# One hybrid decoder layer: the order of the recurrence heads and the distance of the attention's score runs are changed

## The chip, the cores and the metric

The kernel runs on one NeuronCore of a Trainium2 chip. The metric is the device time of one execution in microseconds (us). Three runs of the kernel before gave 470.46, 470.69 and 470.61 us, median 470.61 us. Five engines work side by side: TensorE (PE: matmuls into PSUM, its weight loads shown as PEld), VectorE (DVE), ScalarE (ACT), GpSimd (POOL) and SyncE (SP). Each takes its instructions in a fixed order and waits at the head of its queue.

## The reference

One layer on 512 tokens of width 1024. The normalised input goes through one wide projection, whose columns feed two branches.

- **Attention** (`aq`, `ak`, `av`, `ag`): 8 heads of 64. Queries and keys are normalised per head; scores get a bias that depends on the distance, then a causal softmax. With 512 tokens and blocks of 256, a query sees every earlier key, so that all causal keys count. The result is gated with `silu(ag)`.
- **Recurrence** (`bq`, `bf`, `bi`, `bg`): 4 heads with keys and values of 128. The sigmoid-like forget gate gives a log decay per token and channel; `cum` is its running sum. In chunks, with decay handled inside each score:

```python
    o_inter = jnp.einsum('bhtk,bhkv->bhtv', qc * jnp.exp(cum), state)
    scores = jnp.einsum('bhtk,bhsk,bhtsk->bhts', qc, kc, jnp.exp(diff))
    o_intra = jnp.einsum('bhts,bhsv->bhtv', scores, vc)
    state = state * jnp.exp(last[:, :, 0, :, None]) + jnp.einsum('bhsk,bhsv->bhkv', kc * jnp.exp(last - cum), vc)
```

  The output is normalised per head and gated with `silu(bg)`.

Each branch is projected up to 1024 columns, the two are merged with the sigmoids of `gate_a` and `gate_b`, projected once more and added to the input; then a gated embedding is added.

## The kernel before, in words

**Numbers.** Every product of two fp32 operands is made as three matmuls in a faster fp32 form: both operands are split into a high and a low part (`split`, lines 192 to 194: ScalarE writes the high part, VectorE the difference), and high-high, high-low and low-high are added up. The weights are loaded in blocks, split two blocks ahead of their use (`LD = 2`), and there are two raw buffers and three of each part.

**The order on TensorE is written out.** The program's order is TensorE's order (`manual_schedule`). The other engines' orders come from the scheduler's own simulation; `in_order` marks a few VectorE operations that keep the program's order among themselves, and `high_priority(offset=AHEAD)` moves others forward. The main sequence is the projections: values `bi`, `av`, head 0's `bf` and `bq`, then `aq`, `ak`, then the list `ORDER` (gate blocks `bg`, `ag`, `ga`, `gb` and the other heads' `bf`, `bq`), ending in eight blocks `ub` (up-projection of the recurrence, L252); then `ua` (of the attention), `h` (output projection), `g` and `pe` (gated embedding).

**Side work between the products.** The recurrence and the attention are Python generators. A clock `now` in planned us advances by 0.681 for three matmuls of 512 columns (`tick`) and by `cost` for side work. A generator yields a distance in us or a condition, and goes on at the first tick at which this is met. So the yields decide between which products a step stands on TensorE.

**The recurrence of one head.** `hgrn_gates` makes keys, queries and `cum` behind the head's two projections. `hgrn_intra` (from L484) makes the scores inside chunks of 128. They are cut into levels: for blocks of size b, decayed tiles `hx` (function `kq`, on VectorE and ScalarE, with a yield of `HP = 2.5` after each) hold keys times a decay up to a middle point and queries times a decay from it. A first stage multiplies levels 64, 32, 1 and 16 into the PSUM banks `lpb` and `lpa`; a second stage multiplies levels 8, 4 and 2 into the same `lpa`. Ahead of each stage stands `beside_attention`: it waits until the attention has issued its next run of scores, or 30 us. Masks then gather the levels into the tile `sc`. `hgrn_out` (L591) transposes decayed keys (`hktp`, copied to `hkt` at L599), multiplies them with the values to states' increments (`hds`, L604), makes the states `st` on VectorE, and adds the output in the bank `hop` (L617 and L619). From there VectorE and ScalarE make `ho`: square, sums over the columns, inverse square root, scaling (L624 to L626). `hgrn_gated` multiplies with the gate and splits into `ybh` and `ybl`, which `ub` reads. `ub0` multiplies heads 0 to 3 in this order, three matmuls each. In `recurrence`, head h runs through `hgrn_intra` and `hgrn_out`; only then does head h+1 begin its `kq` tiles.

**PSUM.** Eight banks: three for tag `mm` (projections), three for `a` (scores), two for `g`, which serve `lpb`, `lpa`, `hktp`, `hds` and `hop` of all heads.

**The attention.** For each pair of heads there are two steps: step 0 handles the query blocks 0, 1 and 2, step 1 block 3. `scores` multiplies queries and keys (L708). VectorE adds the bias and finds the row's extreme (L720), ScalarE takes the exponential (L722) and scales (L724), VectorE transposes in 32 by 32 blocks (L727), and 16 DMAs from SP's queue (L738) sort the blocks into the transposed probabilities. These tiles lie in one buffer `pb` of eleven tiles: probabilities in 0 to 2, transposed ones from 3, sorted ones from 6 (step 0) and from 9 (step 1). `out_values` multiplies the sorted probabilities of both steps with the values into the bank `o` (L751), behind the scores of the next pair's step 0. `PACE` is the planned distance from one step's scores to the next: 14 behind step 0 and 27 behind step 1.

Of the kernel before, what the change touches and what calls it, by code (L numbers as in the profile page):

```python
# [28 lines left out]
LEVELS = (16, 8, 4, 2, 1)  # L29

STEPS = ((0, 1, 2), (3,))
PACE = (14.0, 27.0)

HP = 2.5
H0 = 8.0
# [22 lines left out]
def hybrid_layer_kernel(  # L58
# [23 lines left out]
    ctx.enter_context(tc.manual_schedule(engines=ENG))  # L82


    BUFS = {"w": 2, "wh": 3, "wl": 3, "A": 16, "X": 16, "YB": 8, "H": 12, "T": 3, "Q": 4, "KT": 2, "SG": 4, "VV": 8, "s32": 1, "st": 1, "ps": 8}

    def unit(tag, name, dt=F32, shape=(128, 512)):
        return sb.tile(list(shape), dt, tag=tag, bufs=BUFS[tag], name=name)
# [12 lines left out]
    def spawn(gen, after=0.0):  # L101
        sides.append([now[0] + after, gen])
# [44 lines left out]
            xr.append(t)  # L147


    pb = cst.tile([128, 11, 512], F32, name="pb")  # L150
    xfirst = pb[:, 0, 0:272]
    raw0 = unit("w", "wf0", shape=(128, 2, 512))
    A.preload_act_table_set("natural_log_exp_and_others")
# [329 lines left out]

    def hgrn_intra(h):  # L484
        kb, q, cum = hg[h]
        lpb = bank("g", f"lpb{h}").rearrange("p (l c t) -> p l c t", l=4, c=NT)
        big = lpb[:, 2:4].rearrange("p l c t -> p (l c t)").rearrange("p (c t) -> p c t", c=NT)

        def kq(b):

            x = unit("Q", f"hx{h}_{b}")
# [46 lines left out]
        k16 = kq(16)  # L538
        yield HP
        yield from beside_attention()  # L540
        lpa = bank("g", f"lpa{h}").rearrange("p (l c t) -> p l c t", l=4, c=NT)

        for c in range(NT):
# [46 lines left out]
    def hgrn_out(h, vb):  # L590
        kb, q, cum, kd = hg[h][:4]  # L591
        nk = 3 * 128
        yield 1.0
        kt = bank("g", f"hktp{h}")
        for c in range(3):
            PE.transpose(kt[:, c * 128:c * 128 + 128], kd[:, c * 128:c * 128 + 128], ident)
        cost(0.33)
        kts = unit("KT", f"hkt{h}")
        A.activation(kts[:, :nk], kt[:, :nk], AF.Copy)  # L599
        yield 2.5  # L600
        hv = slice(h * 128, h * 128 + 128)
        dsp = bank("g", f"hds{h}")
        for c in range(3):
            PE.matmul(dsp[:, c * 128:c * 128 + 128], kts[:, c * 128:c * 128 + 128], vb[c][:, hv],  # L604
                      start=True, stop=True)
        cost(0.65)
        st = unit("st", f"st{h}", shape=(128, 3, 128))
        V.tensor_copy(st[:, 0], dsp[:, 0:128])
        for c in (1, 2):
            e = c * 128 + 127  # L610
            V.scalar_tensor_tensor(st[:, c], st[:, c - 1], cum[:, e:e + 1], dsp[:, c * 128:c * 128 + 128],
                                   op0=OP.mult, op1=OP.add)
        yield 3.0
        op_ = bank("g", f"hop{h}")
        for c in range(NT):
            s_ = slice(c * 128, c * 128 + 128)
            PE.matmul(op_[:, s_], vb[c][:, hv], sc[:, c, :], start=True, stop=(c == 0))  # L617
            if c:
                PE.matmul(op_[:, s_], st[:, c - 1], q[:, s_], start=False, stop=True)  # L619
        cost(1.5)  # L620
        o = unit("YB", f"ho{h}")
        y = unit("Q", f"hy{h}")
        t = unit("Q", f"ht{h}")
        A.activation(t, op_, AF.Square)  # L624
        token_spread(y, token_factor(token_sums(t, unit("Q", f"htr{h}"), 1.0 / 128)))
        V.scalar_tensor_tensor(o, op_, ogain[:, h:h + 1], y, op0=OP.mult, op1=OP.mult)  # L626
        hg[h] += (o,)

    def hgrn_gated(h, sbg, res):
# [6 lines left out]
        res.append((h_, l_))  # L636
        done.add(f"yb{h}")

    def recurrence(vb, sbg, res):
        for h in range(GH):  # L640
            yield lambda: h in hg
            if h == 0:
                yield H0
            yield from hgrn_intra(h)
            yield from hgrn_out(h, vb)
            spawn(hgrn_gated(h, sbg, res))
            yield HP


    def qk_norm(name, banks, g, res):  # L650
        hs = [unit("A", f"{name}h{i}", R) for i in range(HPAIRS)]
        ls = [unit("A", f"{name}l{i}", R) for i in range(HPAIRS)]
        raws = []
        ss = cst.tile([128, NT, HEADS], F32, name=name + "ss")
        y = cst.tile([128, NT, HEADS], F32, name=name + "y")
        t_ = cst.tile([128, NT, HEADS], F32, name=name + "t")
        for t in range(NT):
            raw = pb[:, (0 if name == "q" else 4) + t]
            A.activation(raw, banks[t], AF.Copy)
            sq = pb[:, 8 + (t + (name == "k")) % 3]  # L660
            A.activation(sq, raw, AF.Square)
            V.tensor_reduce(ss[:, t], sq.rearrange("p (h d) -> p h d", h=HEADS), axis=AX.X, op=OP.add)
            raws.append(raw)
        V.tensor_scalar(ss, ss, 1.0 / 64, None, op0=OP.mult)
        rsqrt(y, t_, ss)
        for t in range(NT):
            r3 = raws[t].rearrange("p (h d) -> p h d", h=HEADS)
            V.tensor_tensor(r3, r3, y[:, t, :, None].to_broadcast([128, HEADS, 64]), op=OP.mult)
        yield 14.0
        for i in range(HPAIRS):  # L670
            tp = bank("a", f"{name}tp{i}")
            for t in range(NT):
                PE.transpose(tp[:, t * 128:t * 128 + 128], raws[t][:, i * 128:i * 128 + 128], ident)
            cost(0.44)
            with tc.high_priority(offset=AHEAD):
                scale_split(hs[i], ls[i], tp, g)
            res.append((hs[i], ls[i]))
            yield 1.3
        done.add(name)

    def attention(qn, kn, va, sags, res):
# [4 lines left out]
        def tiles(step):  # L686
            return 2 + (len(STEPS[step]) > 1)

        P0, Z0, PT0 = 0, 3, (6, 9)

        def scores(hp, step, T):
            (qh, ql), (kh, kl) = qn[hp], kn[hp]
            nt = tiles(step)

            sps = [bank("a", f"s{hp}{step}{i}") for i in range(nt)]
            extra = bank("mm", f"s{hp}{step}x") if nt > 2 else None

            def where(qb, j):
                b_, o = place(qb, j)
                return (extra, 0) if (qb, j) == (1, 1) else (sps[b_], o)  # L700

            for qb in STEPS[step]:
                nk = 128 * (qb + 1)
                for i in range(3):
                    for j in range(2):
                        js = slice(64 * j, 64 * j + 64)
                        b_, o = where(qb, j)
                        PE.matmul(b_[:, o:o + nk], (qh, ql, qh)[i][js, qb * 128:qb * 128 + 128], (kh, kh, kl)[i][js, :nk],  # L708
                                  start=(i == 0), stop=(i == 2))
            cost(sum(3 * max(0.107, (qb + 1) * 0.0538) for qb in STEPS[step]))  # L710
            z = pb[:, Z0:Z0 + nt].rearrange("p t f -> p (t f)").rearrange("p (b t f) -> p b t f", b=4, t=nt)
            with tc.high_priority(offset=AHEAD):
                left = [sum(place(qb, j)[0] == b for qb in STEPS[step] for j in range(2)) for b in range(nt)]
                for qb, j in [(qb, j) for qb in STEPS[step] for j in range(2)]:
                    b_, o = place(qb, j)
                    nk = 128 * (qb + 1)
                    p_ = pb[:, P0 + b_, o:o + nk]
                    st = unit("ps", f"ps{hp}{qb}{j}", shape=(128, 4))
                    s_, so = where(qb, j)
                    in_order(V.tensor_tensor_reduce(p_, s_[:, so:so + nk], T[j][:, nk - 1::-1], -1.0, 3e38,  # L720
                                                    OP.add, OP.min, st[:, 0:1]))
                    A.activation(p_, p_, AF.Exp, bias=st[:, 0:1], scale=-1.0, accum_out=st[:, 1:2])  # L722
                    V.reciprocal(st[:, 2:3], st[:, 1:2])
                    A.activation(p_, p_, AF.Copy, scale=st[:, 2:3])  # L724
                    left[b_] -= 1
                    if left[b_] == 0:
                        V.transpose(z[:, :, b_, :].rearrange("p b (n c) -> p b n c", c=32),  # L727
                                    pb[:, P0 + b_].rearrange("p (n b c) -> p b n c", b=4, c=32))
            return z

        def sorted_groups(step, z):
# [37 lines left out]
        for n in range(len(steps) + 1):  # L769
            if n >= 1:  # L770
                yield PACE[steps[n - 1][1]]
            if n < len(steps):
                hp, i = steps[n]
                if i == 0:
                    for j in range(2):
                        t = unit("T", f"bias{hp}{j}")
                        row = ed[2 * hp + j:2 * hp + j + 1, :]
                        nc.sync.dma_start(t, bass.AP(tensor=row.tensor, offset=row.offset,
                                                     ap=[[1, 128], [1, 512]]))
                        T[hp, j] = t  # L780
                z = scores(hp, i, [T[hp, 0], T[hp, 1]])
            if n >= 1 and steps[n - 1][1] == NS - 1:
                ho = steps[n - 1][0]
                while f"ag{ho}" not in done:
                    yield lambda: f"ag{ho}" in done
                out_values(ho, [pts.pop(n - NS + i_) for i_ in range(NS)])
            if n < len(steps):
                pts[n] = sorted_groups(i, z)
            runs[0] += 1
        runs[0] += 1000  # L790

# [242 lines left out]
```

## Time and profile before

| what | value |
|---|---|
| median of 3 runs | 470.61 us |
| the profiled execution, its own time | 470.31 us |
| its span, first to last instruction | 468.5 us |
| granted TensorE clock, mean | 0.992 |
| TensorE busy | 458.0 us (98%) |
| VectorE busy | 298.8 us (64%) |
| ScalarE busy | 277.0 us (59%) |
| `hop` of heads 1, 2, 3 at | 195.6, 259.7, 307.5 us |
| `ub0` begins at | 313.2 us |

The profile is of one execution. Some 1.8 us of its time lie outside the span. A row of a timeline gives start, duration, engine, line, operation, output and inputs; a bracket at its end gives the idle time just before it and what ended that. The duration of a matmul is longer than the distance to the next, since matmuls overlap. A row of the view by stretches gives the stretch, its length, busy time and number of instructions of each engine shown, then the granted clock, the share of the DMA engines and GB/s.

### The profile page before, as it was taken

Reading aid. Unit: us, or ns where it says so; the run is one execution under the profiler, and the core shown is the slowest. Engines: PE = TensorE matmul, PEld = TensorE weight load, DVE = VectorE, ACT = ScalarE, POOL = GpSimd, SP = SyncE. Lnnn points to the kernel's source line nnn. Section 1 sums busy time; section 2 is a strip of 40 time slices with the busy share of each in tenths; the row PEclk is TensorE's granted clock in tenths of the full one; section 3 lists DMA queues with packets and bytes.
Section 4 is the critical chain, followed back from the end, with each engine's and each line's share of the span. In section 5 each row is a group of like instructions: output and inputs, shape, how many; then the busy total and the mean of one; then the engine's idle time right before and its main releaser. Section 6 shows DMA issues by size and latency. Waiting matters only on the chain.

```text
span 468.5 us, 8111 instructions
## 1 busy us (share of the span) xinstructions
PE 458.0 (98%) x3106; PEld 378.3 (81%) x3106; DVE 298.8 (64%) x604; ACT 277.0 (59%) x532; POOL 38.4 (8%) x77
## 2 busy tenths in 40 slices
PE   9999999999999999999998999997999999999996
PEld 8888888788888888878886888776888788888886
DVE  5668684868798874679495499434559844554222
ACT  5758564657689985888697689763325522232201
POOL 0000100100000010001000000000111100000000
PEclk9999999999999999999999999997999999999999
DMA  7732233222322642344326331631233544322211
GB/s 249 280 99 92 96 128 91 91 91 71 111 80 69 190 138 91 92 123 153 108 67 192 105 112 45 186 110 45 77 104 136 200 145 152 105 86 100 91 45 45
DMA packets 23590, 53.72 MB, mean 115 GB/s; under 512 B 4352, under 2 KB 9728, under 8 KB 23552
## 3 DMA queue, kind: packets, MB, share of 16 engines
q0 software_dynamic: 9056, 32.51, 21.2%
q1 hardware_dynamic: 14352, 20.70, 14.5%
q8 instruction: 24, 0.39, 0.3%
q14 instruction: 14, 0.11, 0.1%
q10 hardware_dynamic: 144, 0.01, 0.0%
HBM read 45.86 MB, written 2.10 MB: 102 GB/s over the span
## 4 chain that ended last, share of the span: by engine, by line
PE 75%; issue 14%; DMA 4%; ACT 4%; DVE 2%; POOL 1%; POOLq 0%; ACTq 0%; DVEq 0%
PE g L252 9%; PE h L252 8%; PE ga L252 6%; PE ub L252 5%; PE ak L382 5%; PE aq L382 5%; PE av L382 5%; PE gb L252 5%; PE bi L382 4%; PE bf L252 4%; PE bq L252 4%; PE bg L252 2%; PE pe L252 2%; PE ag L252 2%; DMA wf<-in_w_tr_dram 2%
## 5 line engine op out<-in xcount | busy, mean ns | idle before, releaser
L193 ACT ACTIVATE wh<-wf 128x1024 fp32r<-128x1024 f32 (+1 forms) x78 | 75.6, 970 | 103.7 <-PE g L252 20.9
L194 DVE TENSOR_TENSOR wl<-wf,wh 128x1024 fp32r<-128x1024 f32 (+1 forms) x78 | 86.5, 1110 | 57.9 <-ACT wh L193 54.1
L226 POOL DMA_DIRECT2D wf<-in_w_tr_dram x30 | 15.8, 528 | 175.1 <-DVE wl L194 152.6
L252 PE MATMUL g<-hh,wh 128*128 128x512 f32 (+1 forms) x72 | 26.3, 366 | 0.0
L252 PE MATMUL g<-hl,wh 128*128 128x512 f32 (+1 forms) x72 | 26.3, 366 | 0.0
L252 PE MATMUL g<-hh,wl 128*128 128x512 f32 (+1 forms) x72 | 26.3, 366 | 0.0
L252 PE MATMUL ga<-xh,wh 128*128 128x512 f32 x64 | 25.7, 402 | 0.0
L252 PE MATMUL gb<-xh,wh 128*128 128x512 f32 x64 | 25.2, 394 | 0.0
L252 PE MATMUL h<-ml,wh 128*128 128x512 f32 x64 | 25.0, 391 | 0.1
L252 PE MATMUL ga<-xl,wh 128*128 128x512 f32 x64 | 25.0, 391 | 0.0
L252 PE MATMUL ga<-xh,wl 128*128 128x512 f32 x64 | 25.0, 390 | 0.0
L252 PE MATMUL gb<-xh,wl 128*128 128x512 f32 x64 | 24.9, 390 | 0.0
L252 PE MATMUL gb<-xl,wh 128*128 128x512 f32 x64 | 24.9, 389 | 0.0
L252 PE MATMUL h<-mh,wh 128*128 128x512 f32 x64 | 24.9, 389 | 0.0
L252 PE MATMUL h<-mh,wl 128*128 128x512 f32 x64 | 24.9, 389 | 0.0
L722 ACT ACTIVATE pb<-pb,ps 128x128 f32<-128x128 f32 (+3 forms) x32 | 17.6, 552 | 10.6 <-DVE ps L720 10.6
L720 DVE CUSTOM_DVE_ANT_0 pb<-s,bias 128x128 f32<-128x128 f32 (+3 forms) x28 | 12.8, 496 | 10.4 <-PE s L708 10.4
L921 DVE TENSOR_TENSOR hf<-h,xres 128x512 f32<-128x512 f32 x8 | 5.5, 692 | 18.0 <-PE h L252 18.0
L252 PE MATMUL ub<-ybh,wh 128*128 128x512 f32 x32 | 13.7, 428 | 3.4 <-ACT ybh L193 3.4
L724 ACT ACTIVATE pb<-pb,ps 128x128 f32<-128x128 f32 (+3 forms) x32 | 15.7, 550 | 0.0
L500 ACT ACTIVATE hx<-hx 128x512 f32<-128x512 f32 x24 | 14.6, 622 | 1.4 <-DVE hx L499 1.3
L252 PEld LDWEIGHTS g<-hh,wh 128*128 128x128 f32 x72 | 13.6, 189 | 2.2
(343 smaller groups left out, 1257.3 us busy)
## 6 DMA issues: line engine op xcount, KB each, us to landing
wf<-in_w_tr_dram POOLq DMA_DIRECT2D x30, 512.0 KB, 3.8
wf<-in_w_tok_dram POOLq DMA_DIRECT2D x8, 512.0 KB, 4.5
wf<-in_w_up_dram POOLq DMA_DIRECT2D x16, 256.0 KB, 2.9
wf<-in_w_o_dram POOLq DMA_DIRECT2D x8, 512.0 KB, 3.7
wf<-in_w_g_dram POOLq DMA_DIRECT2D x8, 512.0 KB, 3.6
wf<-in_w_tok_dram SPq DMA_DIRECT2D x6, 512.0 KB, 3.6
pb<-pb SPq DMA_DIRECT2D x64, 48.0 KB, 2.3
bias<-in_ed_dram SPq DMA_DIRECT2D x8, 256.0 KB, 3.4
```

The lines of the kernel that those rows point to most:

```text
L193: A.activation(hi, src, AF.Copy)
L194: V.tensor_tensor(lo, src, hi.bitcast(F32), op=OP.subtract)
L226: (G if len(wraw) >= FAR else nc.sync).dma_start(raw, ap)
L252: PE.matmul(ps, a[:, k, :], b[k], start=(n == 0), stop=(n == tot - 1))
L382: PE.matmul(banks[t], a[:, s_], b[:, kk, :], start=(k == 0 and i == 0), stop=(k == KD - 1 and i == 2))
L500: A.activation(x, x, AF.Exp)
L720: in_order(V.tensor_tensor_reduce(p_, s_[:, so:so + nk], T[j][:, nk - 1::-1], -1.0, 3e38, OP.add, OP.min, st[:, 0:1]))
L722: A.activation(p_, p_, AF.Exp, bias=st[:, 0:1], scale=-1.0, accum_out=st[:, 1:2])
L724: A.activation(p_, p_, AF.Copy, scale=st[:, 2:3])
L921: V.tensor_tensor(t, ps, xres, op=OP.add)
```

## The change

Four things are changed.

1. `recurrence` no longer runs `hgrn_out` of head h ahead of head h+1. It starts a side generator `hgrn_rest` (output and gating) when `hgrn_intra` of head h is done, and goes on with head h+1 after 2.5. The bank `lpb` is taken where the first stage is issued, not at the start of the head.
2. The yield between the transposes `hktp` and the products `hds` is 4.0, not 2.5.
3. The square of the output is written to `o`, and the other temporary is one tile `N` of its own, in place of three tiles of the tag `Q`.
4. `PACE` is 20 and 21. `scores` now only issues the matmuls; the rest is a function `softmax` of its own, issued behind `out_values` of the pair before. The buffer `pb` has nine tiles; step 1's transposed probabilities lie in 2 and 3, its sorted ones in 4 and 5; the squares of the query and key norms use tiles 8, 4, 5 and 8, 0, 1.

The core of the diff:

```diff
-PACE = (14.0, 27.0)
+PACE = (20.0, 21.0)
...
-    pb = cst.tile([128, 11, 512], F32, name="pb")
+    pb = cst.tile([128, 9, 512], F32, name="pb")
...
     def hgrn_intra(h):
         kb, q, cum = hg[h]
-        lpb = bank("g", f"lpb{h}").rearrange("p (l c t) -> p l c t", l=4, c=NT)
-        big = lpb[:, 2:4].rearrange("p l c t -> p (l c t)").rearrange("p (c t) -> p c t", c=NT)
...
         yield from beside_attention()
+        lpb = bank("g", f"lpb{h}").rearrange("p (l c t) -> p l c t", l=4, c=NT)
+        big = lpb[:, 2:4].rearrange("p l c t -> p (l c t)").rearrange("p (c t) -> p c t", c=NT)
...
         A.activation(kts[:, :nk], kt[:, :nk], AF.Copy)
-        yield 2.5
+        yield 4.0
...
         o = unit("YB", f"ho{h}")
-        y = unit("Q", f"hy{h}")
-        t = unit("Q", f"ht{h}")
-        A.activation(t, op_, AF.Square)
-        token_spread(y, token_factor(token_sums(t, unit("Q", f"htr{h}"), 1.0 / 128)))
+        y = unit("N", f"hy{h}")
+        A.activation(o, op_, AF.Square)
+        token_spread(y, token_factor(token_sums(o, y, 1.0 / 128)))
...
+    def hgrn_rest(h, vb, sbg, res):
+        yield from hgrn_out(h, vb)
+        yield from hgrn_gated(h, sbg, res)
+
     def recurrence(vb, sbg, res):
...
             yield from hgrn_intra(h)
-            yield from hgrn_out(h, vb)
-            spawn(hgrn_gated(h, sbg, res))
+            spawn(hgrn_rest(h, vb, sbg, res))
             yield HP
...
-            sq = pb[:, 8 + (t + (name == "k")) % 3]
+            sq = pb[:, ((8, 4, 5) if name == "q" else (8, 0, 1))[t % 3]]
...
-        P0, Z0, PT0 = 0, 3, (6, 9)
+        Z0, PT0 = (3, 2), (6, 4)
...
-                z = scores(hp, i, [T[hp, 0], T[hp, 1]])
+                where = scores(hp, i)
             if n >= 1 and steps[n - 1][1] == NS - 1:
...
             if n < len(steps):
-                pts[n] = sorted_groups(i, z)
+                pts[n] = sorted_groups(i, softmax(hp, i, [T[hp, 0], T[hp, 1]], where))
```

More of the change, by code (lines that the diff above doesn't have):

```diff
@@ L82, in hybrid_layer_kernel @@
     ctx.enter_context(tc.manual_schedule(engines=ENG))
-    BUFS = {"w": 2, "wh": 3, "wl": 3, "A": 16, "X": 16, "YB": 8, "H": 12, "T": 3, "Q": 4, "KT": 2, "SG": 4, "VV": 8, "s32": 1, "st": 1, "ps": 8}
+    BUFS = {"w": 2, "wh": 3, "wl": 3, "A": 16, "X": 16, "YB": 8, "H": 12, "T": 3, "Q": 4, "KT": 2, "SG": 4, "VV": 8, "s32": 1, "st": 1, "N": 1, "ps": 8}
     def unit(tag, name, dt=F32, shape=(128, 512)):
@@ L687, in tiles, with scores @@
             return 2 + (len(STEPS[step]) > 1)
-        P0, Z0, PT0 = 0, 3, (6, 9)
-        def scores(hp, step, T):
+        Z0, PT0 = (3, 2), (6, 4)
+        def scores(hp, step):
             (qh, ql), (kh, kl) = qn[hp], kn[hp]
@@ L710, in scores, with softmax @@
             cost(sum(3 * max(0.107, (qb + 1) * 0.0538) for qb in STEPS[step]))
-            z = pb[:, Z0:Z0 + nt].rearrange("p t f -> p (t f)").rearrange("p (b t f) -> p b t f", b=4, t=nt)
+            return where
+        def softmax(hp, step, T, where):
+            nt = tiles(step)
+            z = pb[:, Z0[step]:Z0[step] + nt].rearrange("p t f -> p (t f)").rearrange("p (b t f) -> p b t f", b=4, t=nt)
             with tc.high_priority(offset=AHEAD):
@@ L716, in scores @@
                     nk = 128 * (qb + 1)
-                    p_ = pb[:, P0 + b_, o:o + nk]
+                    p_ = pb[:, b_, o:o + nk]
                     st = unit("ps", f"ps{hp}{qb}{j}", shape=(128, 4))
@@ L727, in scores @@
                         V.transpose(z[:, :, b_, :].rearrange("p b (n c) -> p b n c", c=32),
-                                    pb[:, P0 + b_].rearrange("p (n b c) -> p b n c", b=4, c=32))
+                                    pb[:, b_].rearrange("p (n b c) -> p b n c", b=4, c=32))
             return z
```

## The prediction

> **What bounds the kernel now.** I read the page's busy line first, then the waits of TensorE, then its instructions in order of time around each wait.
>
> ```profile
> span 468.5 us, 8111 instructions
> PE 458.0 (98%) x3106; PEld 378.3 (81%) x3106; DVE 298.8 (64%) x604; ACT 277.0 (59%) x532; POOL 38.4 (8%) x77
> ```
> ```profile
> PE ub L252 <- ACT ybh L193: 3.4, 1, 3.4
> PE hds L604 <- ACT hkt L599: 2.3, 3, 1.6
> PE warm L160 <- PEq L1022: 0.8, 1, 0.8
> ```
>
> TensorE is busy all but 10.5 us. The waits (total, times, longest) name 5.7 us of that inside the work; 0.8 us is the start, and the rest is the tail behind the last matmul. No count of matmuls changes, so the change can win these 5.7 us and whatever the clock loses through them, and it can add waits. The longer wait, by start of the matmuls:
>
> ```profile
> 315.04 0.39 PE L252 MATMUL ub<-ybh,wl 128*128 128x512 f32 x1
> 318.82 0.79 PE L252 MATMUL ub<-ybh,wh 128*128 128x512 f32 x1 [3.40 <-ACT ybh L193]
> 324.32 0.39 PE L252 MATMUL ub<-ybh,wh 128*128 128x512 f32 x1
> ```
> ```profile
> 316.00:318.00 2.00, 0.00 (x0) 0.84 0.54 161
> 318.00:320.00 2.00, 1.18 (x2) 0.50 0.00 0
> 324.00:326.00 2.00, 2.00 (x10) 0.95 0.26 98
> 254.00:256.00 2.00, 0.54 (x4) 1.00 0.72 250
> ```
>
> The second fence is TensorE's busy time by stretches of 2 us, with the granted clock behind the count. The matmuls at 318.82 and 324.32 are twelve apart. At the full pace of 0.227 us (a block of 24 takes 5.44 us in the chain row quoted below) the first would have started at 315.27 and the thirteenth at 317.99; it started at 324.32. So this wait costs **6.33 us**: 3.55 of standing and 2.78 of a clock at 0.50. The clock fell about 1.9 us after the last matmul ended at 315.43 (0.84 of 316 to 318 means 0.64 us at half), whereas the 1.57 us wait at 254 to 256 left it at 1.00. The Trainium skill (TensorE: Matmul & The Clock Gate, Part 1: The HAM clock gate) gives about 3.4 us of idleness before the clock halves, with a free-running window. This trace has it halved sooner; the measurement decides how I price a new wait below.
>
> What ends that wait is head 3 of the recurrence, the last one:
>
> ```profile
> 307.53 0.60 PE L617 MATMUL hop<-sc,biv 128*128 128x128 f32 x4
> 308.87 0.39 PE L619 MATMUL hop<-ha,st 128*128 128x128 f32 x2
> ```
> ```profile
> 117.08 5.44 PE ag L252 x24
> ...
> 316.62 0.76 DVE ho L626
> 317.41 0.70 DVE bg3s L632
> 318.14 0.64 ACT ybh L193
> ```
>
> From the first output matmul `hop` at 307.53 to the end of `ybh` it is 11.25 us: square, column sums, inverse root, scaling, gate, split. The planner's clock counts nothing for this, so `ub0` was issued as if `ybh3` were there.
>
> **The change: the order of the heads.** The place of each step on TensorE follows from the program's own clock: `tick(0.681)` for three matmuls, `cost` for side work, and the yields. I added these up by hand; a yield is served at the next tick. The first stage (`lpb`, `lpa`) and the second stage (the three other `lpa` levels) each wait for the next scores of the attention. Planned times (us):
>
> | step | before | after |
> |---|---|---|
> | pair 1, step 1 scores | 195.67 | 202.48 |
> | head 1 `hop` | 190.77 | 192.81 |
> | head 2 first stage | 226.19 (pair 2, step 0) | 203.13 (pair 1, step 1) |
> | head 2 second stage, `hop` | 240.97, 250.19 | 227.39, 237.97 |
> | head 3 first stage | 270.66 (pair 3, step 0) | 248.29 (pair 2, step 1) |
> | head 3 second stage, `hop` | 285.45, 294.67 | 272.54, 283.13 |
> | `ub0` | 300.25 | 300.25 |
> | last `o` | 312.51 | 314.56 |
>
> Before, head 2 starts its four first tiles (2.5 each) only behind head 1's output, at 194.8, and misses the scores at 195.67. After, it starts 2.5 behind head 1's second stage (182.23 planned), has its tiles by 196.8, and meets the scores at 202.48. Head 3 gains likewise: its second stage now goes with pair 3's step 0, and `hop` follows 13.2 later (1.13 + 1.5 for `o`, 0.75, 1.0, 0.33, 4.0, 0.65, 3.0, and roundings). The plan is a fair measure: it puts `ub0` 5.58 behind `hop` 3, the trace 5.7.
>
> So `hop` 3 comes 11.5 us earlier against `ub0`. The fourth product of `ub0` needs `ybh3` some 17.1 + 2.05 = 19.2 us after `hop`; the chain takes 11.25. About 8 us are to spare: **-6.33**. The last `o` moves 2 us later, still 9 us ahead of `ua0`.
>
> **The longer yield before `hds`.** 2.5 becomes 4.0; with the roundings the planned gap from `hktp` to `hds` is 4.41 instead of 3.05.
>
> ```profile
> 250.65 0.49 PE L596 MATMUL hktp<-ident,hkd 128*128 128x128 f32 x3
> 255.46 0.94 PE L604 MATMUL hds<-biv,hkt 128*128 128x128 f32 x6 [1.57 <-ACT hkt L599]
> ```
>
> The worst of the three gaps was 4.81 us, 3.24 without its wait. 3.24 + 1.36 = 4.60 leaves 0.2 of the 2.3 us: **-2.1** (bounds -2.3 and -1.0, should the softmax of step 0 delay the `hkt` copy by a further microsecond).
>
> **Two banks for two heads.** Tag `g` has two banks. While `hop` of head h holds one until `ho` is written, `lpb` of head h+1 has the other, and its `lpa` must wait. TensorE goes in program order, so all products queue behind it. Before, 20 planned us and more lay between (table: 250.19 to 270.66). After, planned, 8.17 (12 products) lie between the end of `hop` and the scores, for heads 1 to 2 and 2 to 3 alike; then come the scores and the first part of the stage:
>
> ```profile
> 153.17 0.50 PE L708 MATMUL s<-kh,qh 64*128 64x512 f32 x2
> 154.07 0.43 PE L546 MATMUL lpb<-hx 128*32 128x64 f32 x16
> 155.13 0.61 PE L521 MATMUL lpa<-hx 128*32 128x16 f32 x32
> ```
>
> That is 8.17 + 0.90 + 1.06 = 10.1 us. What the bank needs, from three rows of `ho` against the end of `hop`:
>
> ```profile
> 196.98 0.39 PE L619 MATMUL hop<-ha,st 128*128 128x128 f32 x2
> 260.99 0.39 PE L619 MATMUL hop<-ha,st 128*128 128x128 f32 x2
> ```
> ```profile
> 205.06 0.69 DVE L720 CUSTOM_DVE_ANT_0 pb<-s,bias 128x512 f32<-128x512 f32 x1
> 207.02 0.74 DVE L626 SCALAR_TENSOR_TENSOR ho<-hop,sm,hy 128x512 f32<-128x512 f32 x1
> 269.69 0.42 DVE L499 TENSOR_TENSOR hx<-hu 128x256 f32<-128x256 f32 x1
> 271.03 0.74 DVE L626 SCALAR_TENSOR_TENSOR ho<-hop,sm,hy 128x512 f32<-128x512 f32 x1
> ```
>
> 10.4 us for heads 1 and 2, 8.1 for head 3 (309.26 to 317.38). Bounds for each hand-over: no wait (8.1), and 1.5 (10.4 plus two score reductions of about 0.6 ahead of `ho`). The nearest rows give 0.3; since the next head's tiles now also lie beside this chain I take 0.5, between them and the middle: **+1.0** for two. The Trainium skill (Perfetto Trace Analysis, Optimization Strategy) says that a gap repeating on the engine that should be full can mean too little PSUM for the next tile; that would be just this wait, and no run here shows it yet.
>
> **Scores 20 and 21 apart, fewer probability tiles.** The scores of step 1 come later against the next pair, so `o` has less time for the 16 DMAs that sort its probabilities. Planned, `o` starts 23.41 after the scores of step 1; with the trace's durations of the side work 24.4, for the last pair 22.0. The issues on SP's queue, and time to landing:
>
> ```profile
> 149.30 11.14 SPq L738 DMA_DIRECT2D pb<-pb  x16
> ...
> 164.23 10.10 SPq L738 DMA_DIRECT2D pb<-pb  x16
> ...
> 214.98 10.65 SPq L738 DMA_DIRECT2D pb<-pb  x16
> ...
> 261.45 3.19 SPq L738 DMA_DIRECT2D pb<-pb  x5
> ...
> 302.23 10.94 SPq L738 DMA_DIRECT2D pb<-pb  x16
> ```
> ```profile
> DMA to landing us min/median/max: 1.8/2.3/5.7
> ```
> ```profile
> 200.75 0.50 PE L708 MATMUL s<-kh,qh 64*128 64x512 f32 x2
> 247.32 0.50 PE L708 MATMUL s<-kh,qh 64*128 64x512 f32 x2
> 296.12 0.50 PE L708 MATMUL s<-kh,qh 64*128 64x512 f32 x2
> ```
>
> From scores to landed: 23.5, 27.2, 19.6 and 19.4 us for pairs 0 to 3. Pair 0 was held by step 0's DMAs, issued until 160.44 and landed at 162.7, which read tiles that its transposes write; its own start only at 164.23. With 20 between the scores they are done in time. Pair 1's second reduction ran at 205.06, 4.3 us behind the scores, in the middle of head 1's chain on VectorE. Three of four fit, so I take 0; the bound is 27.2 - 24.4 = 2.8 for one pair. The aliased tiles (step 1's sorted tiles over step 0's transposed ones, its transposed ones over the third probability tile) ask for the same DMAs to be done within some 23 us: covered by the same rows, and 1 to 4 us of VectorE if not. Issuing `o` ahead of the softmax, the in-place square and the reused square tiles of the key norm change no count: 0, hidden beside the projections.
>
> **Sum** against the profiled execution: 470.31 - 6.33 - 2.1 + 1.0 = 462.9; the median of the runs lies 0.3 above that execution, so **463.2 us**. With no new wait at all it would be 462.0.
>
> **Rivals.** *New waits eat a part.* A pair as late as pair 1 (+2.8) and both hand-overs at their bound (+2.0 more): 468.0 at most; half of it, 465.6, is its time. For it: 27.2 us stands in the trace. Against: it is one row of four. By the rule of the Trainium skill quoted above, such a 2.8 us wait leaves the clock alone. By the fall after 1.9 us in this trace it may cost as much again. *Slower: VectorE and ScalarE fall behind at the hand-over.* Output chain, softmax of step 0 and four tiles of the next head now follow one set of scores.
>
> ```profile
> 180.00:200.00 20.00, 19.73 (x231) 16.40 (x231) 12.36 (x36) 14.14 (x35) 1.58 (x3) 1.00 0.32 97
> 200.00:220.00 20.00, 20.00 (x91) 16.06 (x90) 17.21 (x41) 16.59 (x35) 1.59 (x3) 1.00 0.39 116
> ```
>
> Four tiles are about 16 VectorE operations at 0.34 apart, 5.4 us; 12.36 + 5.4 = 17.8 of 20 us in a stretch like 180 to 200. If the weights' low parts come late by 3.5 us at both hand-overs, each with 2.8 us of half clock, that is +12.6: 475.8, slower than before from 7.4 us of new waits on. Against: 17.21 busy us in the next stretch left TensorE at 20.00, and weights are split two blocks (10.9 us) ahead. *It doesn't do what it says:* the wait at `ub` is also one for its weights, and stays; only `hds` is won: 470.6 - 2.1 + 1.5 (the hand-overs at the middle of their bounds) = 470.0. Against: the later `ub` blocks run without a wait.
>
> **Chances.** Forecast 0.62 (its own range 461.8 to 464.8), eaten part 0.24, slower 0.09, nothing 0.05. The range 461.8 to 468.0 takes in the first two with their bounds. Faster by over 0.2% (0.9 us, about what a measurement can tell): 0.62 + 0.24 + 0.02 = 0.88; within 0.03; slower 0.09.
>
> **What would show it.** Right: no wait of `ub` for `ybh`, a granted clock of 1.00 through `ub`, head 3's `hop` some 17 us before `ub0`, `hds` waits below 0.3. Wrong: a wait of `lpa` on `ho` above 1.5, of `o` on a DMA, or of a product on `wl`; and the forecast falls if `hop` 3 still goes with pair 3's step 1.

## The result and the profile after

| | before | after |
|---|---|---|
| median of the runs compared | 470.53 us (469.68 to 470.69, 4 runs) | 463.83 us (462.19 to 464.26, 4 runs) |
| ratio, 95% interval | | 0.9855 (0.9827 to 0.9883) |
| the profiled execution, its span | 470.31, 468.5 us | 463.43, 461.7 us |
| granted TensorE clock, mean | 0.992 | 0.998 |

The kernel became faster by 1.4%. The forecast was 463.2 us. (Medians and ratios below leave out one execution, of `softmax_first`, which took 667.65 us at a mean granted clock of 0.652.) First the engines' busy time after, then TensorE's waits (total, times, longest):

```profile
PE 454.5 (98%) x3106; PEld 375.9 (81%) x3106; DVE 297.7 (64%) x604; ACT 276.3 (60%) x532; POOL 38.5 (8%) x77
...
```
```profile
PE h L252 <- DVE ml L194: 0.8, 1, 0.8
...
PE hds L603 <- ACT hkt L598: 0.6, 1, 0.6
PE h L252 <- ACT mh L193: 0.5, 1, 0.5
PE o L757 <- DMA pb<-pb: 0.3, 1, 0.3
PE bi L382 <- DVE wl L194: 0.2, 1, 0.2
```

The wait of `ub` for `ybh`, 3.4 us before, is gone; that of `hds` went from 2.3 to 0.55 us. `lpa` waits nowhere. New are small waits: of `o` for its DMAs, 0.2 us in the early block `bi`, and 1.3 us in the first block `h` of the output projection. TensorE's order around the old wait, and a stretch with the granted clock behind the count:

```profile
293.49 0.60 PE L616 MATMUL hop<-sc,biv 128*128 128x128 f32 x4
...
311.18 0.39 PE L252 MATMUL ub<-ybh,wh 128*128 128x512 f32 x1
```
```profile
314.00:316.00 2.00, 2.00 (x11) 1.00 0.64 189
```

`hop` of head 3 stands 17.7 us ahead of `ub0` (5.7 before), and the clock stays at 1.00 where it was at 0.50.

The two profiled executions are 6.88 us apart. The `ub` wait with its half clock gives 6.33 (priced in the prediction), `hds` 1.76, together 8.1; `h`, `o` and `bi` take back 1.3 + 0.3 + 0.2 = 1.8. That leaves 6.3. Of the other 0.6 us, 0.46 lie at the start: the first matmuls of the profile take longer for a longer time before (first row) than after (second row), so that the first matmul of 512 columns starts at 7.07 us before and at 6.61 after.

```profile
5.61 0.63 PE L413 MATMUL bi<-wh,gh 128*128 128x256 f32 x2
```
```profile
5.61 0.44 PE L413 MATMUL bi<-wh,gh 128*128 128x256 f32 x2
```

The start differs from execution to execution: in the two repeats of the changed kernel the same matmul starts at 6.17 and 6.44 us. It lies at 6.79 to 7.07 in the three profiles with the old order of the heads, and at 5.77 to 6.63 in the others. Whether the change has a part in it is not shown, and the prediction has no term for it. For the last 0.2 us the traces name no wait.

### The profile page after: what moved, and what is told of

Same layout as the page of the kernel before. It is cut to its first block, busy times and chain, and to the rows that moved or that the text cites. A ratio compares the mean times of both kernels' runs of the same rounds, so it can differ in the third digit from the quotient of the medians.

```text
span 461.7 us, 8102 instructions
## 1 busy us (share of the span) xinstructions
PE 454.5 (98%) x3106; PEld 375.9 (81%) x3106; DVE 297.7 (64%) x604; ACT 276.3 (60%) x532; POOL 38.5 (8%) x77
## 4 chain that ended last, share of the span: by engine, by line
PE 86%; DMA 5%; ACT 5%; issue 2%; DVE 1%; SPq 1%; POOL 0%; POOLq 0%; DVEq 0%; ACTq 0%
PE ga L252 10%; PE g L252 9%; PE gb L252 9%; PE h L252 8%; PE bq L252 5%; PE ak L382 5%; PE ub L252 5%; PE aq L382 5%; PE bf L252 5%; PE bg L252 4%; PE av L382 4%; PE bi L382 4%; PE ag L252 3%; PE pe L252 2%; DMA wf<-in_w_tok_dram 2%
## 5 line engine op out<-in xcount | busy, mean ns | idle before, releaser
L252 PEld LDWEIGHTS g<-hl,wh 128*128 128x128 f32 x72 | 13.6, 189 | 2.2
L252 PEld LDWEIGHTS g<-hh,wl 128*128 128x128 f32 x72 | 13.6, 189 | 2.2
```

What stands on the lines that cost most here:

```text
L252: PE.matmul(ps, a[:, k, :], b[k], start=(n == 0), stop=(n == tot - 1))
```

## The experiments

Lines of waits give total, times and longest. Times are compared as ratios to the kernel before, timed in the same batch on the same chip. There were three batches: A with `after_again`, `old_pace`, `yield_only` and `near_scores` (before: 471.27 us), B with `yield_back`, `softmax_first`, `third_raw` and `third_raw_hkt` (470.71 us), and C with the last four (470.78 us).

### The changed kernel again: `after_again` and `after_third`

No edit; batches A and C.

> The changed kernel once more. Its profiled execution stood 1.33 us in the first block `h`, behind the high and low parts of the last merged tiles, whose engines had waited for one block of weights that landed 5.4 us after its issue (4.1 us before the change). Theory A: that landing time varies from execution to execution; the wait in `h` is then a different one (0 to 2 us) and the times spread over some 2 us, while `ub` (no wait), `hds` of head 1 (0.5) and `o` of pair 1 (0.3) stay. Theory B: the order of the instructions fixes it; then 1.3 us again and a spread below 0.5 us.

> The changed kernel a third time, on the same chip as the three runs above, for comparison with the third raw buffer: 463.5 us; waits of 0.55 us at `hds`, 0.3 to 0.5 at `o` and 0.8 to 1.5 at `h`, none of `lpa` and `ub`. If the landing times alone make the wait at `h`, it is a third value again.

463.55 us (463.48 to 463.90), ratio 0.9838 (0.9802 to 0.9875), and 463.33 us (462.40 to 465.38), ratio 0.9855 (0.9832 to 0.9878). The waits of `h` in `after_again`, then in `after_third`:

```profile
PE h L252 <- DVE ml L194: 0.8, 1, 0.8
```
```profile
PE h L252 <- DVE ml L194: 0.8, 1, 0.8
...
PE h L252 <- ACT mh L193: 0.6, 1, 0.6
```

The wait in `h` was 1.3, 0.8 and 1.4 us in three executions, that of `hds` 0.55 to 0.57, that of `o` 0.3, 0.5 and 0.3. So one part of `h` returns every time, and another comes and goes; the spread over 2 us was seen in the first and third set of runs and not in the second. Neither theory holds alone. The new order and the new distances aren't needed for it: `yield_only`, below, which has the old ones, stands in `h` as well.

### Old distance, new order: `old_pace`

```diff
-PACE = (20.0, 21.0)
+PACE = (14.0, 27.0)
```

> All of the change, but scores 14 and 27 apart as before. Theory A (the gain is that each head's first tiles are ready when the next scores come): on the planned clock head 2's tiles are ready at 196.1, 0.4 behind pair 1's scores at 195.67, so heads 2 and 3 stand where they stood before, `hop` 3 comes 4.2 planned us ahead of `ub0` (5.6 before, 17.1 in the changed kernel), `ub` waits 3.4 + 1.4 = 4.8 us and its clock halves; the `hds` waits are gone: 470.3 - 2.3 + 1.4 = 469.4 us. Theory B (the overlap of two heads brings the gain by itself): about 464 us, no wait of `ub`.

471.04 us, ratio 0.9998 (0.9977 to 1.0019): nothing is left of the gain. TensorE's rows and waits:

```profile
200.30 0.50 PE L709 MATMUL s<-kh,qh 64*128 64x512 f32 x2
...
232.41 0.43 PE L545 MATMUL lpb<-hx 128*32 128x64 f32 x16
...
306.69 0.60 PE L616 MATMUL hop<-sc,biv 128*128 128x128 f32 x4
...
319.42 0.79 PE L252 MATMUL ub<-ybh,wh 128*128 128x512 f32 x1 [6.19 <-ACT ybh L193]
```
```profile
PE hds L603 <- ACT hkt L598: 1.1, 2, 0.6
```

Head 2's first stage did not go with pair 1's scores at 200.30, which it missed by 0.4 planned us, but with the next ones, at 232.41. All the rest follows as in the kernel before. Theory A holds, though 1.1 us of waits of `hds` stayed, where the theory had none. The wait of `ub` is larger than the 4.8 us expected, since the chain from `hop` to `ybh` took 12.7 us (306.69 to 319.4) in place of 11.25.

### New distance, old order: `pace_only`

```diff
-PACE = (14.0, 27.0)
+PACE = (20.0, 21.0)
```

in the kernel before.

> The kernel before with scores 20 and 21 apart and nothing else. Theory A (the distance is worth something only together with the new order of the heads): head 3's tiles are ready, planned, only when pair 3's step 0 has been issued, so its first stage waits for step 1 and its second for the end of the attention; the products run out at 297 planned us with the last `o`, head 3's second stage and its output still to come. Standing of `o` for its DMAs (about 15 us), of `hds`, `hop` and `ub` (about 13 us), and half clock behind them: about 500 us. Theory B (the distance brings the gain): 464 us.

490.39 us, ratio 1.0422 (1.0395 to 1.0449). The waits:

```profile
PE o L751 <- DMA pb<-pb: 8.3, 1, 8.3
PE ub L252 <- ACT ybh L193: 7.6, 1, 7.6
PE o L751 <- ACT sga L257: 4.2, 1, 4.2
PE hds L604 <- ACT hkt L599: 1.3, 2, 1.0
```

Head 3 falls a step behind and its work stands alone at the end, as theory A says; 21.4 us of standing where some 28 were expected. With `old_pace` this shows that neither the order nor the distance is worth anything without the other: alone they give 0 and +4.2%, together -1.4%.

### The yield before `hds`: `yield_only` and `yield_back`

`yield_only` is the kernel before with

```diff
-        yield 2.5
+        yield 4.0
```

and `yield_back` is the changed kernel with the reverse.

> The kernel before with the yield between `hktp` and `hds` at 4.0 and nothing else. The `hds` waits (2.3 us) go to below 0.3, but `hop` 3 is planned 1.4 us later against `ub0`. Theory A (the two waits trade against each other): `ub` waits 4.8 us instead of 3.4, half clock as before: 470.3 - 2.1 + 1.4 = 469.6 us. Theory B (the 2.3 us are won by themselves): 468.2 us.

> The changed kernel with the yield between `hktp` and `hds` back at 2.5. In its trace the `hkt` copies of heads 1 and 2 ended 5.1 and 4.7 us behind the start of `hktp`, head 3's 2.0; with 2.5 `hds` comes 3.3 us behind it. Theory A (the copies stay where ScalarE's softmax and the next head's tiles put them): waits of 1.9 and 1.4 us in place of 0.55, so 463.5 + 2.7 = 466.2 us. Theory B (the yield no longer matters, since `hop` has time to spare): below 464 us.

`yield_only`: 471.69 us, ratio 1.0014 (0.9989 to 1.0039). `yield_back`: 466.85 us, ratio 0.9913 (0.9887 to 0.9940). The waits of the first, then of the second:

```profile
PE ub L252 <- ACT ybh L193: 6.8, 1, 6.8
PE h L252 <- DVE ml L194: 0.8, 1, 0.8
...
PE hds L604 <- ACT hkt L599: 0.4, 1, 0.4
```
```profile
PE hds L603 <- ACT hkt L598: 3.7, 2, 1.9
```

In the old order the 1.9 us won at `hds` come back at `ub`, and more: `hop` 3 stands 4.3 us ahead of `ub0` (305.98 to 310.31) in place of 5.7, and from there to `ybh` it took 13.3 us in place of 11.25. In the new order, where `hop` has time to spare, going back to 2.5 costs 3.1 us at `hds` (waits of 1.9 and 1.8 us, where 1.9 and 1.4 were expected), and some 3.4 us in time. Theory A holds in both. In the profiled execution of `yield_back` the first of the two waits also cost clock; the last section returns to it.

### The scores nearer to `hop`: `near_scores`

```diff
-PACE = (20.0, 21.0)
+PACE = (16.0, 25.0)
```

> The changed kernel with scores 16 and 25 apart. Heads 2 and 3 still meet the same scores, but these come 4.08 planned us behind the end of `hop` in place of 8.17, so `lpa` is due 6.0 us behind it; the bank is free 8.8 us behind it in the changed kernel. Theory A (two banks bind): `lpa` waits 2.8 us for `ho` at both hand-overs, and the 0.3 us of `o` go: 463.4 + 5.6 - 0.3 = 468.7 us; if the clock falls 1.9 us into a wait as it did at `ub` before the change, up to 2.8 us more for each, to 474. Theory B (the bank is never awaited, since the chain is worked sooner when it is needed sooner): 463.1 us.

477.29 us, ratio 1.0133 (1.0094 to 1.0172): slower than before. TensorE's waits, then VectorE's rows at both hand-overs and the matmul that waited:

```profile
PE lpa L518 <- DVE ho L624: 6.0, 1, 6.0
PE lpa L518 <- DVE s L526: 5.6, 1, 5.6
```
```profile
204.28 0.67 DVE L726 CUSTOM_DVE_ANT_0 pb<-s,bias 128x512 f32<-128x512 f32 x1
...
210.05 0.25 DVE L526 COPY_PREDICATED s<-mkf,lpb 128x64 f32<-128x64 int32 x1
...
212.27 0.75 DVE L624 SCALAR_TENSOR_TENSOR ho<-hop,sm,hy 128x512 f32<-128x512 f32 x1
...
265.01 0.73 DVE L624 SCALAR_TENSOR_TENSOR ho<-hop,sm,hy 128x512 f32<-128x512 f32 x1
```
```profile
210.44 0.63 PE L518 MATMUL lpa<-hx 128*32 128x16 f32 x32 [5.63 <-DVE s L526]
```

The two banks do bind, and much more than the 2.8 us expected. For head 3 `lpa` waits until `ho` of head 2 is written, 12.0 us behind the end of `hop` (253.72 to 265.74). The chain is not of one length: when the scores come early, their reductions and the next tiles' operations stand in the middle of it. For head 2 `lpa` starts at 210.44, just behind the last mask of its own `lpb` (210.30) and before `ho` of head 1 reads `hop` (212.27). So it was given the bank of `lpb`, not that of `hop`: the tag has no third. That is worse in kind, since then it can't start before its own first part is evacuated. Two waits of 11.6 us, each with the clock at half behind it, and the time is over the kernel before.

In the changed kernel the same rows read (PE, then VectorE):

```profile
198.89 0.39 PE L618 MATMUL hop<-ha,st 128*128 128x128 f32 x2
209.34 0.45 PE L518 MATMUL lpa<-hx 128*32 128x16 f32 x32
```
```profile
207.40 0.75 DVE L624 SCALAR_TENSOR_TENSOR ho<-hop,sm,hy 128x512 f32<-128x512 f32 x1
...
209.93 0.68 DVE L726 CUSTOM_DVE_ANT_0 pb<-s,bias 128x512 f32<-128x512 f32 x1
```

`ho` is done at 208.15, 8.9 us behind `hop`; `lpa` is due at 209.34. The reductions come only at 209.93. The margin is 1.2 us.

### The softmax ahead of `out_values`: `softmax_first` and `softmax_first_11`

```diff
-                where = scores(hp, i)
+                z = softmax(hp, i, [T[hp, 0], T[hp, 1]], scores(hp, i))
...
-                pts[n] = sorted_groups(i, softmax(hp, i, [T[hp, 0], T[hp, 1]], where))
+                pts[n] = sorted_groups(i, z)
```

In `softmax_first`, with nine tiles, this writes step 0's transposed tiles over sorted probabilities of the pair before that `out_values` has still to read, so that its attention values are others. `softmax_first_11` has eleven tiles in their old places, and nothing is written over:

```diff
-    pb = cst.tile([128, 9, 512], F32, name="pb")
+    pb = cst.tile([128, 11, 512], F32, name="pb")
...
-        y = unit("N", f"hy{h}")
+        y = kts
...
-        Z0, PT0 = (3, 2), (6, 4)
+        Z0, PT0 = (3, 3), (6, 9)
```

> The changed kernel with the softmax issued ahead of `out_values` again, as before the change. TensorE's order is the same. Theory A (this part is worth nothing): 463.5 us within 0.5, the same waits. Theory B (it keeps the softmax from standing in front of the gating of `o` and the evacuation of `lpa`): `hds` and `lpa` waits grow, 465 us or more.

> The changed kernel with the softmax issued ahead of `out_values`, and eleven tiles with the places they had before, so that nothing that `out_values` still reads is written over; the room comes from the dead `hkt` tile as in the third-buffer kernel. Theory A (the order of the two is worth nothing in itself; the 17 us of waits of `o` in the nine-tile kernel came from the shared tiles alone): 463.6 us within 0.6, no wait of `o` above 0.6. Theory B (the order matters in itself): 465 us or more.

483.99 us, ratio 1.029 (1.0256 to 1.0324), with nine tiles, which neither theory had foreseen; 462.88 us, ratio 0.9841 (0.9815 to 0.9866), with eleven. The waits of `o` in the first, then in the second:

```profile
PE o L757 <- DVE pb L733: 17.1, 3, 5.9
```
```profile
PE o L757 <- DMA pb<-pb: 0.5, 1, 0.5
```

With its own tiles the order of the two makes no difference that these runs can tell (0.9841 against 0.9855 of the changed kernel in the same batch, intervals overlapping). So the new function isn't there for time: it is what lets the tiles be shared.

### A third buffer for raw weights: `third_raw`, `third_raw_hkt`, `third_raw_y47`

```diff
-    BUFS = {"w": 2, ...
+    BUFS = {"w": 3, ...
...
-        y = unit("N", f"hy{h}")
+        y = kts
```

`third_raw_hkt` also issues the copy of `hkt` under `tc.high_priority(offset=AHEAD)`; `third_raw_y47` has `yield 4.7` in place of 4.0 instead.

> The changed kernel with a third buffer for raw weights; the room comes from writing the inverse root of a head's output into the dead `hkt` tile in place of a tile of its own. Each load of weights is issued one block earlier. Theory A (the first block `h` stands because a block of weights lands late): the wait in `h` (0.8 to 1.3 us) goes, 463.5 - 1.0 = 462.5 us. Theory B (VectorE is full there, 18.1 us of 20, and the weights are not what is late): the wait stays, 463.5 us.

> The same, and the copy of `hkt` is put forward on ScalarE by the priority that the softmax has. Theory A: the 0.55 us of `hds` in head 1 go too, 462.0 us. Theory B (the copy only changes places with other work that TensorE waits for): as the run before it, within 0.2.

> The changed kernel with the third raw buffer, and 4.7 in place of 4.0 between `hktp` and `hds`, which moves `hds` and `hop` behind one more product (0.68 us). Theory A: the two `hds` waits (0.56 and 0.39 us) go, and the bank of `hop`, free 8.8 us behind it and now due 9.5 us behind it, is still not awaited: 461.1 - 1.0 = 460.1 us. Theory B (the copies move back with the yield, or `lpa` starts to wait for `ho`): 461.1 us or more.

| kernel | time | ratio to before |
|---|---|---|
| `third_raw` | 461.14 us | 0.9796 (0.9771 to 0.9821) |
| `third_raw_hkt` | 460.98 us | 0.9792 (0.9770 to 0.9814) |
| `third_raw_y47` | 460.35 us | 0.9790 (0.9770 to 0.9811) |
| changed kernel, same batch as the last | 463.33 us | 0.9855 (0.9832 to 0.9878) |

The waits of `third_raw`, `third_raw_hkt` and `third_raw_y47`, one fence each:

```profile
PE hds L603 <- ACT hkt L598: 1.0, 2, 0.6
```
```profile
PE hds L604 <- ACT hkt L599: 1.1, 2, 0.6
```
```profile
PE hds L603 <- ACT hkt L598: 0.4, 1, 0.4
PE o L757 <- DMA pb<-pb: 0.3, 1, 0.3
```

With the third buffer TensorE no longer waits in `h`; `o` still waits 0.3 us in `third_raw_y47`. What happened in `h` in the changed kernel (GpSimd's issue, ScalarE, VectorE, TensorE):

```profile
355.65 0.53 POOL L226 DMA_DIRECT2D wf<-in_w_o_dram  x1 [4.18 <-DVE wl L194]
...
361.07 1.06 ACT L193 ACTIVATE wh<-wf 128x1024 fp32r<-128x1024 f32 x1 [2.12 <-DMA wf<-in_w_o_dram]
362.04 0.61 ACT L193 ACTIVATE mh<-sga 128x512 fp32r<-128x512 f32 x1
...
363.31 0.68 DVE L194 TENSOR_TENSOR ml<-sga,mh 128x512 fp32r<-128x512 f32 x1
364.05 0.50 PE L252 MATMUL h<-ml,wh 128*128 128x512 f32 x1 [0.85 <-DVE ml L194]
```

The weights issued at 355.65 were split only from 361.07, 5.4 us later; before the change it was 4.1 us for the same block. ScalarE and VectorE stood at the head of their queues for them, and behind stood `mh` and `ml`, which TensorE needed. With a buffer more the same load is issued at 350.96 in `third_raw` and split at 357.17, and neither engine stands for it. This is the case of theory A. That `hy` moved into the `hkt` tile isn't the gain: `softmax_first_11` has that with two raw buffers and stays at 0.9841. The batch medians differ by 2.2 us, where 1.0 was expected. Of that the waits name 1.2 (1.4 in `h` and 0.3 of `o` gone, 0.5 more at `hds`), against `after_third`; the rest they don't name. Putting the `hkt` copy forward did nothing: the same ScalarE operations stand ahead of it in the same order as in the changed kernel. Why the priority doesn't move it, these runs don't show. One more product between `hktp` and `hds` takes the wait down to 0.4 us, where nothing was expected to be left; the ratio moves by only 0.0006 beside `third_raw`'s, within the intervals. `third_raw_y47` and the changed kernel, on the same chip, have intervals that don't meet: it beats both kernels.

## Why the prediction was right, point by point

- **What bounds the kernel, and the price of `ub`'s wait** (-6.33): right. The wait and the half clock are gone, and `ub0` to the first `h` is 6.36 us shorter (311.18 to 357.30 after, 313.22 to 365.70 before). The 2.78 us of clock in it are those of the profiled execution, though: in batch A the kernel before shows a mean clock of 0.991 to 0.993 in nine executions, like the profiled one, and of 0.995 or 0.996 in ten, about half the loss. The ten took 470.5 us on average, the nine 471.7.
- **The order of the heads by the planned clock**: right in each row. Head 2 went with pair 1's step 1, head 3's second stage with pair 3's step 0, `hop` 3 17.7 us ahead of `ub0` (17.1 planned). `old_pace` shows how thin this is: 0.4 us of plan decided over the whole gain.
- **`hds`** (-2.1): the mechanism right, the size off: -1.76, and the sign "below 0.3" wasn't met. The waits of heads 1, 2 and 3 were 0.27, 1.57 and 0.47 us; now they are 0.55, 0 and 0. Head 1's grew, since its copy starts 4.65 us behind the start of `hktp`, 2.99 before. The bound had named the softmax of step 0 for such a delay. The trace names the next head's tiles: of the rows ahead of the copy on ScalarE, these three, 1.2 us in all, don't stand there before the change, and a fourth `hx` (at 186.80, 0.5 us) lies between the steps of the softmax:

```profile
189.74 0.42 ACT L502 ACTIVATE hx<-hk 128x256 f32<-128x256 f32 x1
...
190.56 0.62 ACT L497 ACTIVATE hx<-hx 128x512 f32<-128x512 f32 x1
191.09 0.42 ACT L501 ACTIVATE hx<-hx 128x256 f32<-128x256 f32 x1
```

- **Two banks** (+1.0): mis-sized, it measured 0. The 10.4 us came from chains in which the next head's tiles or the reductions lay inside; after the change these come later, and the chain takes 8.9 and 8.7 us. The nearest row was head 3's 8.1. That the banks bind was right all the same, with a margin of 1.2 us (`near_scores`).
- **Scores and `o`** (0): nearly right, +0.3 for pair 1, the pair that the prediction named.
- **Shared tiles and the order of softmax and `out_values`** (0): right as a price in itself, but the step "change no count: 0" missed what the order is for. With shared tiles the old order costs 17 us of waits. The in-place square and the tile `N` were not tested by themselves.
- **The sum** (463.2 against 463.83): that it came so near is in part luck. The +1.0 for the banks wasn't there; 1.3 us in `h` were, in a place that no step looked at; and the start of the profiled execution gave 0.46. The trace of before held a hint: the chain that ended last ran from a load of `w_o` (363.79) through its two split parts and `ml` to `h` at 370.93.
- **The rivals**: "eaten part" came in small (`o`, `h`), "slower" did not come. The two readings of the clock that the first of them weighs, none lost in a 2.8 us wait or some behind 1.9 us, are both too simple: see the last section. VectorE was busy 15.1 of 20 us in 180 to 200, and TensorE waited for no weights there. The supply of weights, doubted for `ub`, was thin, but at `h`.

## What to carry to other kernels

When a step is released by an event that comes at intervals, being ready a little late costs a whole interval: work out who is ready when, before pricing any overlap, and change the order and the interval together. A wait removed upstream is only worth what the next join doesn't give back; `yield_only` won 1.9 us and kept none. What a wait costs in clock depends on where it falls, so it is priced as a range. Sharing buffers turns an order that cost nothing into one that must hold, and a buffer freed is best spent where a load's landing stands in a queue ahead of other work.

## What the runs showed that was not expected

The clock halves after very different times of standing. From the end of the last matmul it took 1.9 us in the kernel before, 4.1 and 3.6 in `near_scores`, 4.7 in `old_pace` and 4.9 in `yield_only`. In `yield_back` it halved 0.8 us after a wait of 1.9 us was over (192.69 to 193.48). The prediction took 1.9 us as if it were the rule.

The rule that fits all these runs counts in steps. The kernel before keeps the half clock for 6.8 us, `yield_back` for 3.4, both `near_scores` waits for 6.8 (208.87 to 215.70 and 263.48 to 270.31), and the two falls there lie 54.61 us apart: two, one, two and sixteen times 3.41 us. So in these runs the clock changes only at ticks 3.41 us apart. The rows are TensorE's stretches from tick to tick (busy time, count, granted clock), of the kernel before, then of `yield_back` around its two waits of 1.92 and 1.75 us:

```profile
313.97:317.37 3.40, 1.45 (x7) 1.00 0.76 228
317.38:320.79 3.41, 1.97 (x4) 0.50 0.01 5
320.80:324.19 3.39, 3.39 (x9) 0.50 0.16 27
324.21:327.61 3.40, 3.40 (x16) 1.00 0.12 47
```
```profile
190.07:193.48 3.41, 1.50 (x11) 1.00 0.06 15
193.49:196.89 3.40, 3.40 (x11) 0.50 0.60 156
241.27:244.68 3.41, 1.66 (x10) 1.00 0.06 14
```

The clock behind the last row is 1.00. In the fourteen profiles, from the first matmul of 512 columns on, every stretch at full clock with at most 1.50 us of matmuls is followed by half clock, and none with 1.66 or more. Half clock ends behind a stretch with at least 2.71 us of matmuls (`pace_only`), and not behind 2.43 or less. So a wait costs clock when it empties more than half of one stretch. One of 1.92 us did, within a single stretch, and one of 1.75 us didn't. The 3.40 us of the kernel before fell into two stretches and left 1.45 us in the first. Where the ticks fall differs from execution to execution, and so does the price.

The Trainium skill (TensorE: Matmul & The Clock Gate, Part 1: The HAM clock gate) speaks of a free-running window of about 3.4 us, which these ticks bear out. For the fall it asks for an idle window; here windows with 1.45 and 1.50 us of matmuls were enough, and the measurement decides. Back to full speed it took 4.4 to 5.4 us from the first matmul in `near_scores` (265.89 to 270.31) and the kernel before (318.82 to 324.20), more than the Trainium skill's 3.4 us: the first stretch was too empty to count, as the 1.97 us above show, and the next had to end.
